# Later places for layer 1's gate products, and activations stored cell by cell in DRAM

## The chip, the cores and the metric

The kernel runs on one core of a Trainium2 chip. The metric is the device time of one execution in microseconds (us); lower is better. The core has a matrix engine (PE, with its weight loads shown as PEld), a vector engine (DVE), an activation engine (ACT), a general engine (POOL) and a sequencer that issues all transfers of this kernel (SP). Sixteen DMA engines carry the transfers between DRAM and the on-chip memory.

## The reference, cut to what matters

Two layers of a streaming encoder run over 2048 prompt frames and 32 sample frames of width 1024, all in f32.

```python
# layer 0
h  = rms_norm(x, ln_pre[0])
qa, ka, va, ga, qb, kb, vb, gb = split(h @ w_in_ab)        # 3328 columns
oa = window_attention(rope(qa), rope(ka), va, sinks)       # own 64-frame chunk + 2 before
ob = band_attention(qb, kb, vb, relpos)                    # own chunk + 8 before
x2 = x + rms_norm(concat(oa * silu(ga), ob * silu(gb)) @ w_out_ab, ln_post[0])
# layer 1
xb, z = split(rms_norm(x2, ln_pre[1]) @ w_in_c)            # 2048 columns
xc = causal_conv4(xb)
r  = sigmoid(blockdiag(xc, wa) + ba);  gi = sigmoid(blockdiag(xc, wx) + bx)   # the gates
a  = exp(8 * r * log_sigmoid(lam))
hs = scan(h[t] = a[t] * h[t-1] + sqrt(1 - a[t]**2) * gi[t] * xc[t])
y  = x2 + rms_norm((hs * silu(z)) @ w_out_c, ln_post[1])
```

Besides `y` the kernel returns the key, value, convolution and scan states.

## The kernel before, in words

**Data.** Activations lie transposed: the 1024 features are 8 groups (k) of 128 partitions, the frames run along the free axis. The 2084 columns (2048 prompt, 4 of padding, 32 sample) are cut into six blocks of 352 columns (the last has 324), and three parts `b` = 0, 1, 2 of two blocks each. Every f32 operand of a large product is split into a high and a low piece (`r0h`/`r0l`, `r1h`/`r1l` for activations, `wh`/`wl` for weights), so one output tile `acc` of 128 features by one block takes 8 x 3 = 24 matmuls.

**Stages.** Input projection of layer 0 for the three parts, with the attention of earlier parts mixed in; output projection of layer 0 (`out_part`, about 990 to 1180 us in the profile); then layer 1, part by part: `in_part` (16 weight tiles by two blocks, with gates, scan and so on), followed by its `out_part`. The last `out_part` ends the program.

**Cells.** Norms and residuals work on cells, half a block wide: 176 columns (162 in the last block). `norm_proc` loads cells of the input (`xT`) or of layer 0's result (`x2T`), squares them on ACT, reduces on DVE, sums over partitions by two matmuls into `misc`, and writes the high and low pieces. `fin_out` follows each `acc` of an output projection: ACT writes the scaled `acc` into the buffer `m` (two buffers, each 8 k by 352 columns) and its square, DVE adds the squares into `sacc`; after the eighth, `m` is multiplied by the norm factor `r`, the residual cell (loaded by `res_load` into `xr`, `eti` or `xt`) is added, and the cell goes to DRAM: to `x2T` in layer 0, to `yT` in layer 1. A buffer `m` is free for the next block only when these stores have landed. In DRAM `xT`, `x2T` and `yT` are matrices of 1024 rows by 2084 columns, so a cell of 176 columns is 1024 pieces of 704 bytes (`x_load`, and the stores in `add`).

**Gates.** In `in_part`, for each of eight feature groups `c`, `fin_x` copies `acc` to `xb`, DVE makes the convolution, ACT or DVE and DVE make the split operands `xs` (two tiles, one for each half of 128 features), and PE multiplies each by the gate weights `gh`, `gl` into `g` (4 matmuls for each tile). ACT takes tanh of `g`, then exp and sqrt; DVE continues to the scan. The waits are on rings of one or two buffers, so the channels follow one another.

**What sets the order.** The order of every engine's instructions is made at build time by a list scheduler (`Sched`). Each step is a generator that yields a request `R(engines, inputs, rings)`; the scheduler keeps estimated times for each engine, each tile (`sch.w`), the transfers (`dma_us`, from the length of the contiguous runs) and takes a step when its inputs are estimated ready. On the chip every engine runs its list strictly in order and waits on semaphores. So an estimate never makes a wait by itself; it decides what stands in front of what. SP issues in one list, too.

**Output weights of the last part.** The last `out_part` runs block by block, so that each weight tile is read twice from DRAM (`wh<-wo1s`, `wl<-wo1s`, 512 KB each, three buffers of each); its 16 tiles of 24 matmuls are the end of the program, but for the last norm.

Of the kernel before, what the change touches and what calls it, by code (L numbers as in the profile page):

```python
# [12 lines left out]
OP = mybir.AluOpType  # L13
# [3 lines left out]
KT = 8  # L17
# [35 lines left out]
WIN = 3.4133  # L53

# [346 lines left out]
def hybrid_kernel(ctx, tc, I, O):  # L401
# [30 lines left out]
    oT, zT, x2T = dt("oT", [D, TOK]), dt("zT", [D, TOK]), dt("x2T", [D, TOK])  # L432
# [191 lines left out]
    def split_R(xt, w, ri, col, ins=()):  # L624

        hh, hl = RT[ri]
        cs = slice(col, col + w)
        yield R("A", [xt] + list(ins))
        A.copy(hh[:, :, cs], xt[:, :, :w])
        th = sch.t["A"] + 0.13  # L630
        ends = []
        for ks in (slice(0, 4), slice(4, 8)):
            e, _ = yield R(("V", "G"), [lambda: th], cost=(0.8, 1.63))
            ENG[e].tensor_tensor(hl[:, ks, cs], xt[:, ks, :w], f32(hh[:, ks, cs]), OP.subtract)
            ends.append(sch.t[e] + 0.13)
        return max(ends)
# [29 lines left out]
    def norm_proc(src, b, gi, ri, key, rings, free=None, after=None, src_ready=(), then=None, blocks=(0, 1), hold=None):  # L666
# [5 lines left out]
        def block(bi, xs):  # L672
            cc = cells[2 * bi:2 * bi + 2]
            sa, sb = yield R("A", [xs[0]], [ssr, ssr])
            offs = [0, cc[0][3]]
            tot = cc[0][3] + cc[1][3]
            for x, (_, _, _, w), o in zip(xs, cc, offs):
                for ss, ks in ((sa, slice(0, 4)), (sb, slice(4, 8))):
                    sq, = yield R("A", [x], [sqr])
                    A.activation(sq[:, :, :w], x[:, ks, :w], AF.Square)  # L680
                    yield R("V", [sq])
                    V.tensor_reduce(ss[:, o:o + w], sq[:, :, :w].rearrange("p k t -> p t k"), AX.X, OP.add)
                    sqr.release(sq)
            e, _ = yield R(("G", "V"), [sa, sb], cost=(0.89, 0.43))
            ENG[e].tensor_tensor(sa[:, :tot], sa[:, :tot], sb[:, :tot], OP.add)
            ssr.release(sb)
            ps = yield from norm_sum(sa[:, :tot])
            r = sa
            yield R("A", [ps], func="sqrt")
            A.activation(r[:, :tot], ps[:, :tot], AF.Sqrt, bias=epsT, scale=1.0 / D)  # L690
            psr_.release(ps)
            for x, (_, _, _, w), o in zip(xs, cc, offs):
                yield R("V", [r])
                V.reciprocal(r[:, o:o + w], r[:, o:o + w])
                for k0 in (0, 4):
# [941 lines left out]

    def fin_out(S, c, acc, rel, cs):
        if c == 0:
# [4 lines left out]
        A.activation(S.m[:, c, cs], acc[:, cs], AF.Copy, scale=vec[:, S.gi, c:c + 1])  # L1644
# [16 lines left out]
        blk = 2 * S.b + S.bi  # L1661
# [20 lines left out]
        def add(o, sw, tm):  # L1682

            cc = slice(o, o + sw)
            for ks in parts:
# [28 lines left out]
        for o, sw in pieces:  # L1714
# [11 lines left out]
    def res_load(S):  # L1726
# [3 lines left out]
        if S.cells is LAST:  # L1730

            xa, = yield R("SP", rings=[xtr])
            xb, = yield R("SP", rings=[xrr])
            at = 0
            for o, sw in LAST:
                x = xb if o else xa
                S.xt[o] = x.rearrange("p k t -> p (k t)")[:, at:at + KT * sw].rearrange("p (k t) -> p k t", k=KT)
                at = at + KT * sw if o else 0
                x_load(S.xt[o], S.residual, T0[2 * S.b + S.bi] + o, sw)
# [97 lines left out]
    def in_part(b, base, ri, yi):  # L1837
# [4 lines left out]
        def fin_x(c, bi, acc):  # L1842
# [39 lines left out]
            for h, xt in enumerate(xs):  # L1882
                p_, = yield R("PE", [xt, ("gw", b, c)], [gr[h]])
# [181 lines left out]
def _layout(inputs):  # L2065
# [4 lines left out]
    xT[:, S0:] = a["x_sample"][0].T  # L2070
    nat = lambda n: [i * 128 + np.arange(128) for i in range(n)]
    gw = np.zeros((8, 128, 2, 128), f)
    for c in range(8):
# [22 lines left out]
        "xT": xT,  # L2096
# [15 lines left out]
_OUTS = {"yT": (1024, T0[5]), "yL": (128, KT * BW[5]), "akp": (128, 128), "avp": (128, 128), "bkp": (512, 512), "bvp": (512, 512),  # L2112
# [40 lines left out]
```

## Time and profile before

| | |
|---|---|
| median of 3 runs | 1818.16 us (1817.07 to 1822.6) |
| the profiled execution, its own time | 1822.39 us |
| its span, first to last instruction | 1820.6 us |
| PE busy in the span | 1732.4 us (95%) |
| DVE busy | 1544.3 us (85%) |
| ACT / POOL busy | 990.9 us (54%) / 324.8 us (18%) |
| DMA | 362.79 MB, 16 engines 66% busy on the queue of SP's transfers |
| granted TensorE clock, mean | 0.988 |

Busy times are unions of instruction times. A gap is put down to the engine or transfer that released the waiting instruction. All instructions carry the line of one helper (L103), so groups are told apart by tile names: `acc<-r0h,wh` writes tile `acc` and reads `r0h` and `wh`. The window view gives, for a stretch of time, each engine's busy time with the number of its instructions, the granted clock (1.00 is full), the mean busy share of the 16 DMA engines (it can pass 1 in a short stretch, since a packet counts where it starts) and the bytes moved in GB/s. DMA issues stand under SPq with the time that SP spent issuing.

### The profile page before, as it was taken

The page shows a single profiled execution, that of the slowest core. Times are in us where ns is not written, and L with a number is a line of the kernel's source. Part 1 is how long each engine was busy: PE and PEld are TensorE (multiplying, and loading weights), DVE is VectorE, ACT ScalarE, POOL GpSimd, SP SyncE. Part 2 cuts the span into 40 slices and gives each one's busy share as a digit, 9 for nine tenths or more (in the row PEclk, how much of TensorE's full clock was granted, in tenths as well). Part 3 has the DMA queues.
Part 4 walks back from the last instruction along what each step waited for, and adds up shares of the span by engine and source line. Part 5 has one row for each costly group of instructions (what it writes and reads, how often), then busy time and mean ns, then how long its engine had stood idle before and what let it go on. Part 6 is the DMA issues. An engine that isn't in the chain of part 4 may idle for free. (4 is left out here: it accounts for less than half of the span.)

```text
span 1820.6 us, 31699 instructions
## 1 busy us (share of the span) xinstructions
PE 1732.4 (95%) x11078; PEld 1673.4 (92%) x11078; DVE 1544.3 (85%) x3240; ACT 990.9 (54%) x2029; POOL 324.8 (18%) x283
## 2 busy tenths in 40 slices
PE   8999999999999999999998999998999999999996
PEld 7998999998899999899997999998899999999996
DVE  9899977899998779998887688899998989789844
ACT  4275543377666416666564333457854676437831
POOL 4332204323222233312114000000021000200001
PEclk8999999999999999999999999999999999999998
DMA  5798766888655369877867785785457733564376
GB/s 179 207 250 252 225 190 198 224 217 254 175 162 151 97 183 251 209 210 200 232 161 216 222 215 158 223 281 193 171 211 233 222 124 125 181 215 163 131 254 206
DMA packets 293367, 362.79 MB, mean 199 GB/s; under 512 B 38404, under 2 KB 244152, under 8 KB 293192
## 3 DMA queue, kind: packets, MB, share of 16 engines
q1 hardware_dynamic: 293208, 360.78, 66.2%
q8 instruction: 87, 1.43, 0.3%
q14 instruction: 72, 0.59, 0.1%
HBM read 255.77 MB, written 107.00 MB: 199 GB/s over the span
## 5 line engine op out<-in xcount | busy, mean ns | idle before, releaser
L103 PE MATMUL acc<-r0h,wh 128*128 128x352 f32 (+2 forms) x1832 | 592.9, 324 | 12.2 <-ACT r0h L103 5.6
L103 PE MATMUL acc<-r0l,wh 128*128 128x352 f32 (+2 forms) x1832 | 593.2, 324 | 2.8 <-DVE r0l L103 2.8
L103 PE MATMUL acc<-r0h,wl 128*128 128x352 f32 (+2 forms) x1832 | 592.7, 324 | 1.8 <-DMA wl<-wo1s 1.8
L103 PEld LDWEIGHTS acc<-r0h,wh 128*128 128x128 f32 x1832 | 347.1, 189 | 15.4 <-ACT r0h L103 6.5
L103 PEld LDWEIGHTS acc<-r0l,wh 128*128 128x128 f32 x1832 | 347.6, 190 | 4.9 <-DVE r0l L103 3.8
L103 PEld LDWEIGHTS acc<-r0h,wl 128*128 128x128 f32 x1832 | 347.4, 190 | 3.6 <-DMA wl<-wo1s 2.6
L103 PE MATMUL acc<-r1h,wh 128*128 128x352 f32 (+1 forms) x864 | 278.7, 323 | 3.5 <-ACT tz L103 1.8
L103 PE MATMUL acc<-r1h,wl 128*128 128x352 f32 (+1 forms) x864 | 278.4, 322 | 2.9 <-DVE wl L103 2.9
L103 PE MATMUL acc<-r1l,wh 128*128 128x352 f32 (+1 forms) x864 | 278.1, 322 | 0.0
L103 ACT ACTIVATE pt<-pt,nm 128x256 f32<-128x256 f32 (+6 forms) x272 | 169.7, 626 | 67.5 <-DVE nm L103 65.0
L103 POOL TENSOR_TENSOR wl<-wst,wh 128x1024 fp32r<-128x1024 f32 x41 | 101.7, 2481 | 465.5 <-DMA wst<-wo_in 346.1
L103 ACT CAST pp<-T 128x256 fp32r<-128x256 f32 (+4 forms) x314 | 132.8, 438 | 75.1 <-PE T L103 63.4
L103 PEld LDWEIGHTS acc<-r1h,wh 128*128 128x128 f32 x864 | 163.2, 189 | 4.6 <-ACT tz L103 2.1
L103 PEld LDWEIGHTS acc<-r1h,wl 128*128 128x128 f32 x864 | 163.1, 189 | 3.8 <-DVE wl L103 3.8
L103 POOL TENSOR_SCALAR pt<-pt,rr 128x256 f32<-128x256 f32 (+4 forms) x142 | 98.0, 700 | 384.1 <-DVE rr L103 219.1
L103 PEld LDWEIGHTS acc<-r1l,wh 128*128 128x128 f32 x864 | 163.2, 189 | 0.0
L103 DVE TENSOR_TENSOR pp<-T,pp 128x256 fp32r<-128x256 f32 (+4 forms) x314 | 151.3, 498 | 9.1 <-ACT pp L103 7.3
L103 PE MATMUL T<-ident,pt 128*128 128x128 f32 (+1 forms) x864 | 142.7, 273 | 14.2 <-DVE pp L103 10.8
L103 PE MATMUL O<-pp,vt 128*128 128x256 f32 (+2 forms) x728 | 133.9, 306 | 10.6 <-DVE pp L103 5.4
L103 PEld LDWEIGHTS T<-ident,pt 128*128 128x128 f32 (+1 forms) x864 | 99.9, 139 | 40.7 <-DVE pp L103 17.6
L103 ACT ACTIVATE m<-acc,vec 128x352 f32<-128x352 f32 (+2 forms) x89 | 48.9, 549 | 144.3 <-PE acc L103 138.4
L103 PE MATMUL S<-kk,qa 128*128 128x320 f32 (+5 forms) x376 | 121.3, 337 | 4.1 <-DVE nm L103 2.3
(242 smaller groups left out, 3055.4 us busy)
## 6 DMA issues: line engine op xcount, KB each, us to landing
wst<-w_in SPq DMA_DIRECT2D x93, 512.0 KB, 4.7
wst<-wo_in SPq DMA_DIRECT2D x32, 512.0 KB, 4.3
wh<-w1s SPq DMA_DIRECT2D x32, 512.0 KB, 3.6
wl<-w1s SPq DMA_DIRECT2D x32, 512.0 KB, 4.7
wh<-wo1s SPq DMA_DIRECT2D x24, 512.0 KB, 3.7
wl<-wo1s SPq DMA_DIRECT2D x24, 512.0 KB, 4.6
kk<-kB SPq DMA_DIRECT2D x32, 320.0 KB, 5.1
vt<-vB SPq DMA_DIRECT2D x16, 640.0 KB, 4.8
```

The source lines that it names most:

```text
L103: r = fn(*a, **k)
```

## The change

Two things are changed together. First, a gate's matmuls are offered to the scheduler 1.0 us later than the estimated end of their operand `xs` (`GLATE`). Second, `xT`, `x2T` and `yT` are stored in DRAM by cells, each partition's part of a cell in one piece: a cell of 176 columns is then 128 pieces of 8 x 176 x 4 = 5632 bytes. The two blocks that are loaded first get a copy of their own by blocks (`xF`), with pieces of 2816 bytes in place of 1408. On chip, `m` is laid out cell by cell as well; ACT's write of a whole block into it has two runs of 176 columns, and in the last block, whose cells are now 176 and 148 wide, it becomes two instructions. The last block's residual is loaded as two cells rather than three pieces, and the final sums of its second cell go to another tile (`xt`) than the residual's. The host arranges input and output accordingly.

```diff
+GLATE = 1.0
+SUBS = [[(0, 176), (176, 176)]] * 5 + [[(0, 176), (176, 148)]]
...
+    x2T = dt("x2T", [128, KT * TOK])
...
     def x_load(xt, src, t0, w):
-        SP.dma_start(out=xt[:, :, :w], in_=src[:, t0:t0 + w].rearrange("(k p) t -> p k t", p=128))
+        SP.dma_start(out=flat(xt)[:, :KT * w], in_=src[:, KT * t0:KT * (t0 + w)])
...
-        A.activation(S.m[:, c, cs], acc[:, cs], AF.Copy, scale=vec[:, S.gi, c:c + 1])
+        if cs == slice(0, BLK):
+            A.activation(flat(S.m).rearrange("p (x k t) -> p x k t", x=2, k=KT)[:, :, c], acc[:, cs].rearrange("p (x t) -> p x t", x=2),
+                         AF.Copy, scale=vec[:, S.gi, c:c + 1])
+        else:
+            for o, sw in subs(blk):
+                a, e = max(o, cs.start), min(o + sw, cs.stop)
+                if a < e:
+                    A.activation(m_cell(S.m, blk, a, e - a)[:, c], acc[:, a:e], AF.Copy, scale=vec[:, S.gi, c:c + 1])
...
-                    SP.dma_start(out=S.dst[:, T0[blk] + o:T0[blk] + o + sw].rearrange("(k p) t -> p k t", p=128), in_=m[:, :, cc])
+                    t = KT * (T0[blk] + o)
+                    SP.dma_start(out=S.dst[:, t:t + KT * sw].rearrange("p (k t) -> p k t", t=sw), in_=mc)
...
-                p_, = yield R("PE", [xt, ("gw", b, c)], [gr[h]])
+                tx = sch.w[xt.tensor.name] + GLATE
+                p_, = yield R("PE", [lambda: tx, ("gw", b, c)], [gr[h]])
```

Since both edits change the scheduler's estimates, the order differs from PE's row 657 of 9962 on; three places follow, before and after apart. (The helper's line is L103 before and L106 after.)

**SP's list near the end**, in the last `out_part`: `wo1s_115` and `wo1s_116` are the last two weight tiles, `yT_out<-m` are the two cells of the block before the last, `chp` to `ccs` small states. Before:

```order
L103 DMA yT_out<-m_10500 128x8x176 x2
L103 DMA wh_119<-wo1s_115 128x1024
L103 DMA wl_122<-wo1s_115 128x1024
L103 DMA chp_out<-hcar 128x8
L103 DMA chs_out<-hsmp 128x8
L103 DMA ccp_out<-hist 128x24
L103 DMA ccs_out<-csmp 128x24
L103 DMA wh_120<-wo1s_116 128x1024
L103 DMA wl_123<-wo1s_116 128x1024
L103 DMA xt_151<-x2T 128x8x176
```

After:

```order
L106 DMA wh_119<-wo1s_115 128x1024
L106 DMA wl_122<-wo1s_115 128x1024
L106 DMA chp_out<-hcar 128x8
L106 DMA chs_out<-hsmp 128x8
L106 DMA ccp_out<-hist 128x24
L106 DMA ccs_out<-csmp 128x24
L106 DMA yT_out<-m_10500 128x1408
L106 DMA wh_120<-wo1s_116 128x1024
L106 DMA wl_123<-wo1s_116 128x1024
L106 DMA yT_out<-m_10500 128x1408
L106 DMA xt_151<-x2T 128x1408
```

The two stores of `yT` stood ahead of the last two weight tiles; now one stands behind the first of these and one behind the second.

**PE's list in layer 0's output projection**, where `norm_proc` for layer 1's first block sums its squares (`misc<-xs,onesr`). Before:

```order
L103 MATMUL acc_159<-r1h,wl_124 128x352
L103 MATMUL misc_160<-xs_10567,onesr 128x352 x2
L103 MATMUL acc_159<-r1h,wh_121 128x352
L103 MATMUL acc_159<-r1l,wh_121 128x352
L103 MATMUL acc_159<-r1h,wl_124 128x352
L103 MATMUL acc_159<-r1h,wh_121 128x352
```

After:

```order
L106 MATMUL acc_0_10557<-r1h,wh_121 128x352
L106 MATMUL acc_0_10557<-r1l,wh_121 128x352
L106 MATMUL acc_0_10557<-r1h,wl_124 128x352
L106 MATMUL acc_0_10557<-r1h,wh_121 128x352
L106 MATMUL misc_160<-xs_10567,onesr 128x352 x2
L106 MATMUL acc_0_10557<-r1l,wh_121 128x352
```

The sum stood at row 5802, twelve matmuls before the end of an `acc` tile; it now stands at row 5818, four matmuls into the next tile: 16 rows later.

**PE's list in layer 1, second part**, one channel's gates (`g_0`, `g_1` by the first and second `xs` tile) among the products of the next weight tile. Before:

```order
L103 MATMUL acc_158<-r1h,wl_124 128x352
L103 MATMUL g_0_10559<-xs_10567,gh_10564 128x352
L103 MATMUL g_0_10559<-xs_10567,gl_10565 128x352
L103 MATMUL g_0_10559<-xs_10567,gh_10564 128x352
L103 MATMUL g_0_10559<-xs_10567,gl_10565 128x352
L103 MATMUL acc_0_10557<-r1h,wh_119 128x352
L103 MATMUL acc_0_10557<-r1l,wh_119 128x352
```

After:

```order
L106 MATMUL acc_0_10557<-r1h,wh_119 128x352
L106 MATMUL acc_0_10557<-r1l,wh_119 128x352
L106 MATMUL g_0_10559<-xs_10567,gh_10564 128x352
L106 MATMUL g_0_10559<-xs_10567,gl_10565 128x352
L106 MATMUL g_0_10559<-xs_10567,gh_10564 128x352
L106 MATMUL g_0_10559<-xs_10567,gl_10565 128x352
L106 MATMUL acc_0_10557<-r1h,wl_122 128x352
```

The first four stood at row 7800 and stand at 7808, behind eight matmuls of the next tile; the other four (by `xs_10568`) went from row 7812 to 7824.

More of the change, by code (lines that the diff above doesn't have):

```diff
@@ L431, in hybrid_kernel @@
     vAs, vBs = dt("vAs", [160, 2, 128]), dt("vBs", [544, 8, 128])
-    oT, zT, x2T = dt("oT", [D, TOK]), dt("zT", [D, TOK]), dt("x2T", [D, TOK])
+    oT, zT = dt("oT", [D, TOK]), dt("zT", [D, TOK])
+    x2T = dt("x2T", [128, KT * TOK])
     WSEQ = []
@@ L633, in split_R @@
             e, _ = yield R(("V", "G"), [lambda: th], cost=(0.8, 1.63))
-            ENG[e].tensor_tensor(hl[:, ks, cs], xt[:, ks, :w], f32(hh[:, ks, cs]), OP.subtract)
+            ENG[e].tensor_tensor(hl[:, ks, cs], xt[:, ks], f32(hh[:, ks, cs]), OP.subtract)
             ends.append(sch.t[e] + 0.13)
@@ L697, in block @@
                     for k in range(k0, k0 + 4):
-                        V.scalar_tensor_tensor(x[:, k, :w], x[:, k, :w], vec[:, gi, k:k + 1], r[:, o:o + w], OP.mult, OP.mult)
+                        y = dense(x, w)[:, k]
+                        V.scalar_tensor_tensor(y, y, vec[:, gi, k:k + 1], r[:, o:o + w], OP.mult, OP.mult)
             ssr.release(sa)
@@ L1682, in add @@
         def add(o, sw, tm):
[L1684 removed]
+            mc = m_cell(m, blk, o, sw)
             for ks in parts:
@@ L1730, in res_load @@
         if S.cells is LAST:
+            t0, (_, (ob, wb)) = T0[2 * S.b + S.bi], subs(2 * S.b + S.bi)
             xa, = yield R("SP", rings=[xtr])
-            xb, = yield R("SP", rings=[xrr])
-            at = 0
[L1735 to L1739, printed above, removed]
+            x_load(xa, S.residual, t0, ob)
+            S.xt[0] = dense(xa, ob)
+            S.xk[0] = sch.dma_end
+            xb, xo = yield R("SP", rings=[xrr, xtr])
+            x_load(xb, S.residual, t0 + ob, wb)
+            S.yt = {0: S.xt[0]}
+            at = 0
+            for o, sw in LAST[1:]:
+                S.xt[o] = dense(xb, wb)[:, :, o - ob:o - ob + sw]
+                S.yt[o] = flat(xo)[:, at:at + KT * sw].rearrange("p (k t) -> p k t", t=sw)
+                at += KT * sw
                 S.xk[o] = sch.dma_end
@@ L2095, in _layout @@
     return {
-        "xT": xT,
+        "xT": np.ascontiguousarray(np.concatenate([x3[:, :, T0[i] + o:T0[i] + o + w].reshape(128, KT * w) for i in range(6) for o, w in SUBS[i]], 1)),
+        "xF": np.ascontiguousarray(np.concatenate([x3[:, :, T0[i]:T0[i] + BLK].reshape(128, KT * BLK) for i in range(2)], 1)),
         "w0": _wtiles(a["w_in_ab"][0], _colperm0()),
@@ L2130 @@
     c = np.ascontiguousarray
-    yT = np.concatenate([g["yT"]] + [g["yL"][:, KT * o:KT * (o + w)].reshape(128, KT, w).transpose(1, 0, 2).reshape(1024, w) for o, w in LAST], 1)
+    cell = lambda y, o, w: y[:, KT * o:KT * (o + w)].reshape(128, KT, w).transpose(1, 0, 2).reshape(1024, w)
+    yT = np.concatenate([cell(g["yT"], T0[i] + o, w) for i in range(5) for o, w in SUBS[i]] + [cell(g["yL"], o, w) for o, w in LAST], 1)
     def kT(x, h, n):
```

35 lines of the change are left out of this document (23 added, 12 removed).

## The prediction

> **What bounds the kernel now.** I read the page first, for the engines.
>
> ```profile
> span 1820.6 us, 31699 instructions
> PE 1732.4 (95%) x11078; PEld 1673.4 (92%) x11078; DVE 1544.3 (85%) x3240; ACT 990.9 (54%) x2029; POOL 324.8 (18%) x283
> ```
>
> PE is busy 95% of the span, and its work isn't changed: the same matmuls by the same widths. So the change can only move what PE loses: 1820.6 - 1732.4 = 88 us idle, plus the stretches at a lower clock. What matters is where PE waits and for whom. Next, therefore, the table of waits and the users of `x2T`:
>
> ```profile
> PE g L103 <- DVE xs L103: 8.2, 11, 1.7
> PE acc L103 <- ACT r0h L103: 5.6, 3, 3.5
> ...
> who waited for it (us, times):
>   ACT m L103: 8.7, 3
>   ACT sq L103: 5.8, 2
> ```
>
> The first row is what the later gates aim at: PE waited 11 times, 8.2 us, for the gates' operand. The last rows say that the layout matters too: ACT stood still 8.7 us for stores to `x2T` to free `m`, and 5.8 us for loads from it.
>
> **How fast cells move.** Of a transfer I need the time on all 16 DMA engines, since its followers wait for that where the engines are full. The first two windows hold only 704-byte pieces (loads of `x2T`), the third rows of 5 KB into 64 partitions (`kk<-kB`), the fourth only weight tiles (4 KB in each of 128 partitions), the fifth the first loads, with pieces of 1408 bytes:
>
> ```profile
> 1367.00:1370.00 3.00, 3.00 (x20) 3.00 (x20) 3.00 (x3) 1.09 (x3) 1.17 (x1) 1.00 0.89 177
> 1417.50:1420.50 3.00, 3.00 (x21) 3.00 (x20) 2.80 (x5) 0.81 (x2) 0.00 (x0) 1.00 0.76 222
> 542.00:545.00 3.00, 3.00 (x23) 2.98 (x22) 2.85 (x10) 1.90 (x5) 0.72 (x1) 1.00 0.73 178
> 1750.00:1753.00 3.00, 3.00 (x20) 3.00 (x19) 0.45 (x1) 0.91 (x2) 0.00 (x0) 1.00 0.99 344
> 10.50:13.50 3.00, 3.00 (x11) 2.90 (x11) 3.00 (x4) 1.45 (x2) 3.00 (x4) 0.50 1.06 366
> ...
> wst<-wo_in SPq DMA_DIRECT2D x32, 512.0 KB, 4.3
> x2T<-m SPq DMA_DIRECT2D x10, 704.0 KB, 7.3
> ```
>
> GB/s over share gives the pace of full engines: 199 and 292 for 704-byte pieces, 244 for `kk`, 347 for weights, 345 for the first loads. A cell is 704 KB = 721 kB: 2.5 to 3.6 us now. In pieces of 5632 bytes it should take 2.1 us if it goes like the weights, 3.0 us if like `kk`. I take the weights, whose 128 partitions are those of a cell; `kk` fills 64. So a cell saves 0.4 to 1.5 us, at worst it loses 0.5. From issue to landing the two last rows set 7.3 us for a store against 4.3 us for 512 KB in long pieces; scaled by size that is 4.3 + 192/347 = 4.9 us, about 2.4 us sooner. SP is held up as well:
>
> ```profile
> 1088.84 5.11 SPq L103 DMA_DIRECT2D xt<-x2T  x2
> 1742.57 0.32 SPq L103 DMA_DIRECT2D wh<-wo1s  x1
> 1785.95 3.33 SPq L103 DMA_DIRECT2D wh<-wo1s  x1
> ```
>
> An issue that takes 0.32 us with nothing before it took 3.33 us behind two cells, and two cells took 5.11 us. With 128 pieces for a cell in place of 1024 I expect this to go.
>
> The Trainium skill speaks against the whole edit: by "DMA: Bandwidth & Descriptors", section "Specifications", pieces of 512 bytes or more already run at line rate, so 704 would do. By it the layout's terms below would be zero. The windows above disagree: 199 to 292 against 347.
>
> **Term 1, layer 0's output projection: 9.5 us won.** Windows, then PE's and ACT's instructions with their waits in brackets:
>
> ```profile
> 1100.00:1110.00 10.00, 7.20 (x29) 6.64 (x28) 7.98 (x10) 3.49 (x8) 0.00 (x0) 0.69 0.72 222
> 1150.00:1160.00 10.00, 7.32 (x44) 7.03 (x44) 10.00 (x23) 6.57 (x12) 0.00 (x0) 0.92 0.65 191
> 1160.00:1170.00 10.00, 10.00 (x61) 10.00 (x61) 9.19 (x14) 7.18 (x10) 0.00 (x0) 0.91 0.71 218
> ...
> 1088.20 0.43 PE L103 MATMUL acc<-r1h,wh 128*128 128x352 f32 x1 [1.83 <-ACT tz L103]
> 1104.65 1.22 PE L103 MATMUL misc<-xs,onesr 128*128 128x352 f32 x2 [2.80 <-DVE xs L103]
> 1158.96 0.64 PE L103 MATMUL acc<-r0h,wh 128*128 128x324 f32 x1 [2.68 <-ACT tz L103]
> ...
> 1075.03 0.55 ACT L103 ACTIVATE m<-g,vec 128x352 f32<-128x352 f32 x1 [4.57 <-DMA x2T<-m]
> 1093.95 0.79 ACT L103 ACTIVATE sq<-ex 128x704 f32<-128x704 f32 x1 [3.58 <-DMA ex<-x2T]
> 1145.19 0.56 ACT L103 ACTIVATE m<-g,vec 128x352 f32<-128x352 f32 x1 [3.79 <-DMA x2T<-m]
> ```
>
> Three waits of PE, 7.3 us, each follow a wait of ACT for a store or load of `x2T`, 12 us in all. After two of them the clock is halved for a while: 0.31 x 10 = 3.1 us lost at 1100, (0.08 + 0.09) x 10 = 1.7 us at 1150 to 1170. Together 12.1 us. The first: the store lands about 2.4 us sooner, half of ACT's 4.57, and I count 1.5 of 1.83. The second: PE's list now has the sum 16 rows later, and a full-speed matmul takes 0.165 us (112.85 us for 684, row below), so 2.6 us of the 2.80 go by the order alone, and its load is faster too; with the clock 2.8 + 3.1, I count 5.5. The third depends on a store and then on a weight tile behind the stores; 2.5 of 2.68 + 1.7. Bounds: 2.6 (the place in the list alone, no clock) to 12.1.
>
> **Term 2, the last output projection: 7 us won, 0.7 given back.** Here DMA is the bound:
>
> ```profile
> 1768.00:1771.00 3.00, 1.83 (x7) 1.59 (x8) 1.31 (x3) 1.18 (x1) 0.00 (x0) 0.74 1.03 415
> 1771.00:1774.00 3.00, 3.00 (x16) 3.00 (x16) 1.10 (x1) 0.56 (x1) 0.00 (x0) 0.69 0.31 124
> 1795.00:1798.00 3.00, 2.02 (x8) 1.79 (x9) 0.00 (x0) 0.00 (x0) 0.00 (x0) 0.80 0.93 306
> 1798.00:1801.00 3.00, 3.00 (x16) 3.00 (x15) 0.00 (x0) 0.00 (x0) 0.00 (x0) 0.64 1.12 296
> ...
> 1768.52 0.39 PE L103 MATMUL acc<-r0h,wh 128*128 128x324 f32 x1 [1.59 <-DMA wh<-wo1s]
> 1769.70 0.64 PE L103 MATMUL acc<-r0h,wl 128*128 128x324 f32 x1 [0.66 <-DMA wl<-wo1s]
> 1795.25 0.39 PE L103 MATMUL acc<-r0h,wh 128*128 128x324 f32 x1 [1.82 <-DMA wh<-wo1s]
> 1796.51 0.44 PE L103 MATMUL acc<-r0h,wl 128*128 128x324 f32 x1 [0.73 <-DMA wl<-wo1s]
> ...
> 1807.46 1.25 DVE L103 RECIPROCAL r<-r 128x176 f32<-128x176 f32 x1 [4.45 <-ACT r L103]
> 1808.73 0.33 ACT L103 ACTIVATE r<-misc,epsT 128x84 f32<-128x84 f32 x1 [0.54 <-PE misc L103]
> ```
>
> At 1768 PE waits 2.25 us for a weight tile that two residual cells delayed, and then runs slow: 3 x (0.26 + 0.31) = 1.7 us. Two cells save 0.8 to 3.0 us; I count 1.2, which leaves a wait of 1 us and, I think, the full clock: 2.9. At 1795 it is 2.55 us for the tile that stood behind two stores of `yT` in SP's list, and 3 x (0.20 + 0.36) = 1.7 us of clock. That tile is now ahead of the stores, so all 4.2 should go. What is late next there is the last tile, behind one store: 721 kB at 347 GB/s, 2.1 us, while a tile of 24 matmuls lasts 24 x 0.165 = 4 us, so it is covered. All four gaps whose clock I count, of 2.25 to 2.8 us, were followed by a slow stretch, in all 3.1 + 1.7 + 1.7 + 1.7 = 8.2 us. The Trainium skill's "TensorE: Matmul & The Clock Gate", section "Why this matters for your kernels", has the clock drop only after gaps of some 3 us; by it these stretches would not come from the gaps, and the sum would be up to 8 us less. The trace disagrees, and I go by it.
>
> The tail after PE's end is a chain on DVE. There ACT writes the first 240 columns of `m` in two instructions, the norm's sums stand four short matmuls later, and DVE's second instruction is the reciprocal of the last 84 columns, which needs the ACT result that ended at 1809.06, where DVE was free at 1808.71: 0.35 + some 0.35 us, 0.7 lost. Bounds of the term: 3 to 7.9.
>
> **Term 3, the gates: 3 us won.** Two windows, the gates of the first and of the second part:
>
> ```profile
> 1210.00:1345.00 135.00, 124.55 (x761) 121.17 (x760) 130.08 (x182) 104.05 (x131) 4.82 (x2) 1.00 0.62 213
> 1428.00:1546.00 118.00, 112.85 (x684) 108.97 (x684) 104.85 (x151) 85.81 (x110) 0.00 (x0) 1.00 0.44 143
> ```
>
> A gate moves 4 to 12 rows, 0.7 to 2 us, and the 8.2 us of waits would go. But who waits for a gate: ACT's tanh, then DVE's scan, in line. In the first part DVE is busy 130.08 of 135 us (96%) where PE is at 124.55; a wait taken from PE there comes back at the part's end, where PE already waits for the last `r0h` and `r0l`. In the second part DVE has 11% left (104.85 of 118). I count the waits of the second and third part, some 5 us, less 2 us more at the three ends. Bounds: all 8.2 won; or every one of 24 channels late by 0.7 us and in line, 16.8 lost less 8.2, so 8.6 lost.
>
> **Costed at nothing.** The two-run write of `m` by ACT and the doubled one of the last block, 13 + 2 more instructions of some 0.4 us: ACT is at 54%, and PE has two other `acc` tiles to go to. The first loads, at 345 GB/s already: 0 to 1. The rest of layer 0 is reordered from PE's row 657 on, without a direction that a row would show: 0, with 5 us either way:
>
> ```profile
> 115.00:956.00 841.00, 816.66 (x5462) 778.06 (x5461) 729.71 (x1957) 481.73 (x1197) 219.79 (x210) 1.00 0.72 202
> ```
>
> PE idles 24.3 us there. From the whole I take 2.8 us, since DVE (85%) comes next and will keep something of each wait.
>
> **Sum.** 9.5 + 7.1 - 0.7 + 3 - 2.8 = 16 us. The profiled execution took 1822.4 us (1.8 us outside its span), 4.2 us over the median of the runs; the terms are differences within one execution, and I take them from the median: 1818.2 - 16 = 1802.
>
> **Rivals.** (a) The length of the pieces buys nothing: full engines carry a cell as slowly as before. Then what remains is order: the sum's later place (2.6), the tile ahead of the stores (4.2 - 0.7), the gates (3), and 1 us of SP's time: 1808. The two 704-byte windows and the landing times speak against it. (b) The gates' delay runs through: DVE's line of channels is full, as the 96% says, and the 8.6 us are lost in place of 3 won: 1802 + 11.6 = 1814. The 11% in the second part speak against it. (c) The slower side: the reordered attention. Its operands pass PE, ACT, DVE and PE again, and PE's idle 24.3 us in 115 to 956 could double, if transposes meet products that are not ready; 1802 + 24 = 1826. It decides from 16 us of added idle time; nothing in the rows asks for it, but nothing excludes it. (d) Long pieces go at `kk`'s pace or worse: a cell takes 3.0 us, 0.5 more than the faster of today's windows and 0.6 less than the slower; term 1 falls to 4, the first wait of term 2 stays: 1811.
>
> **How the numbers follow.** My forecast has 56% (1794 to 1809: term 1 and 2 between their bounds, mostly), (a) 15%, (b) 13%, (c) 7%, (d) 7%; 2% lie below 1794. About 0.3%, 5.4 us, is what a measurement of this kernel can tell from no change. Faster takes my case, what lies below it, (a), most of (d) and a third of (b): 0.82; same the rest of (b) and of (d): 0.11; slower is (c): 0.07. The range goes to 1790 below and 1816 above, past (a), (d) and (b).
>
> **What would show it.** Right: no wait of ACT for `x2T<-m` over 2 us, `x2T<-m` and `xr<-x2T` landing within 5 us, no issue of SP over 1 us behind cells, no wait for `wo1s` at the last two tiles, the clock at 1.00 from 1000 us to the end of PE, and PE's waits for `xs` under 3 us. Wrong: cell transfers under 250 GB/s at full share, longer waits for `r0h` at the ends of the parts, or PE idle well over 24 us between 115 and 956 us.

## The result, and the profile after

The changed kernel takes 1810.39 us (median of 5 runs, 1805.5 to 1813.68) against 1818.16 us for the kernel before: ratio 0.9947, 95% interval 0.9928 to 0.9966. So it is faster, by 7.8 us by the medians and 9.6 by the ratio, where 16 were forecast, and the time lies inside the forecast range (1790 to 1816) and 8 us over the forecast itself (1802). The profiled execution is the median one. From its page and its table of waits (in the latter: total us, times, longest):

```profile
span 1808.6 us, 31683 instructions
PE 1726.3 (95%) x11078; PEld 1674.2 (93%) x11078; DVE 1537.9 (85%) x3228; ACT 1001.9 (55%) x2055; POOL 322.1 (18%) x285
...
PE acc L106 <- ACT r0h L106: 10.3, 3, 4.6
PE g L106 <- DVE xs L106: 8.5, 6, 5.0
ACT m L106 <- DMA x2T<-m: 10.2, 3, 9.4
```

PE waits for `xs` about as long as before (8.5 us, where it was 8.2), in 6 waits instead of 11, and for `r0h` 10.3 instead of 5.6 us. Neither the wait for `xs` nor ACT's wait for `m` (10.2 us, where it was 8.7), with which the prediction began, fell. What did fall is seen in layer 0's output projection and at the end. Windows (busy time of PE, PEld, DVE, ACT, POOL, granted clock, DMA share, GB/s), then SP's, ACT's and PE's instructions with their waits in brackets:

```profile
1100.00:1110.00 10.00, 8.62 (x54) 8.32 (x53) 8.36 (x15) 4.58 (x8) 0.00 (x0) 1.00 0.35 125
1150.00:1160.00 10.00, 10.00 (x65) 9.86 (x64) 9.86 (x25) 7.88 (x19) 0.00 (x0) 1.00 0.49 195
1090.00:1092.00 2.00, 2.00 (x15) 2.00 (x14) 1.57 (x4) 0.13 (x1) 0.00 (x0) 1.00 0.99 406
1066.50:1068.50 2.00, 2.00 (x14) 2.00 (x14) 2.00 (x3) 0.00 (x0) 0.00 (x0) 1.00 0.99 299
...
x2T<-m SPq DMA_DIRECT2D x11, 704.0 KB, 4.1
...
1782.95 0.38 SPq L106 DMA_DIRECT2D yT_out<-m  x1
...
1074.48 0.56 ACT L106 ACTIVATE m<-g,vec 128x352 f32<-128x352 f32 x1 [9.36 <-DMA x2T<-m]
...
1105.92 0.43 PE L106 MATMUL misc<-xs,onesr 128*128 128x352 f32 x1 [1.38 <-DVE xs L106]
1789.25 0.38 PE L106 MATMUL acc<-r0h,wl 128*128 128x240 f32 x1 [0.84 <-DMA wl<-wo1s]
```

At 1100 and 1150 us the clock is full, where it was 0.69 and 0.92. Full DMA engines now carry cells at 410 GB/s when they are loaded (406 over 0.99; 199 to 292 before) and at 300 where a store and a load run together (1066.5 us): 1.8 to 2.4 us for a cell. A store lands after 4.1 us instead of 7.3, and its issue takes 0.3 to 0.4 us. Of the waits for the last two weight tiles 0.84 us is left. What got worse most lies in the first part of layer 1:

```profile
1232.90 0.66 PE L106 MATMUL g<-xs,gh 128*128 128x352 f32 x1 [4.99 <-DVE xs L106]
1333.83 0.66 PE L106 MATMUL acc<-r0h,wh 128*128 128x352 f32 x1 [3.90 <-ACT r0h L106]
1335.30 0.66 PE L106 MATMUL acc<-r0l,wh 128*128 128x352 f32 x1 [0.81 <-DVE r0l L106]
...
1230.00:1240.00 10.00, 7.10 (x30) 6.91 (x31) 9.55 (x14) 6.80 (x10) 0.00 (x0) 0.66 0.34 82
1332.00:1342.00 10.00, 7.36 (x29) 6.99 (x30) 7.10 (x7) 4.47 (x8) 2.76 (x2) 0.66 0.36 131
```

One gate waits 4.99 us, the part's end 4.7 us, and after each the clock is halved (these matmuls take 0.66 us each, and the clock's mean over the 10 us is 0.66).

**A ledger for PE.** To compare all profiles I use one number per stage: for each PE instruction the distance from its start to the next one's start, less the median distance for that shape in the profile of before (0.160 us for 352 columns), summed over a stage. I call it the excess; it holds waits and slow clock together. Stages are cut at equal sums of the nominal distances and named by before's times: 91–300 is the early attention, 1006–1183 layer 0's output projection, the next three columns are the parts of layer 1, and the last is the last output projection. In the stages left out, up to 91 and from 300 to 1006 us, all 14 profiles lie within 2.8 and 4.1 us of one another.

| kernel | 91–300 | 1006–1183 | 1183–1384 | 1384–1582 | 1582–1731 | 1731–end | span |
|---|---|---|---|---|---|---|---|
| before, first profile | 11.0 | 14.2 | 13.2 | 9.5 | 4.5 | 11.8 | 1820.6 |
| before, second profile (e8_before) | 9.2 | 9.3 | 13.2 | 9.2 | 4.4 | 9.4 | 1808.1 |
| changed | 14.8 | 2.4 | 19.8 | 8.8 | 2.0 | 3.8 | 1808.6 |
| gates alone (e1_gates) | 8.7 | 10.2 | 12.0 | 8.3 | 3.4 | 5.7 | 1805.7 |
| gates alone, old end (e11_gates_end) | 8.3 | 10.7 | 12.1 | 7.9 | 4.0 | 7.9 | 1806.6 |
| layout alone (e2_layout) | 12.6 | 2.5 | 14.8 | 9.4 | 4.4 | 4.4 | 1806.0 |
| layout, old estimates (e3_oldprice) | 8.7 | 4.9 | 19.2 | 10.0 | 3.7 | 5.7 | 1806.2 |
| new estimates, old layout (e4_order) | 15.3 | 9.0 | 23.0 | 16.2 | 4.1 | 6.4 | 1829.5 |
| before, two stores moved (e10_behind) | 8.1 | 13.5 | 13.2 | 9.5 | 4.1 | 5.4 | 1809.0 |
| changed, two stores moved back (e12_ahead) | 16.6 | 2.3 | 19.7 | 8.5 | 1.8 | 7.5 | 1812.4 |
| changed, old estimates in attention (e5_mix) | 9.2 | 2.5 | 20.1 | 10.5 | 1.8 | 3.9 | 1805.1 |
| changed, gates late in parts 2, 3 only (e6_late_b12) | 13.0 | 3.0 | 14.5 | 9.0 | 2.1 | 4.0 | 1801.5 |
| both of the last (e9_best) | 8.9 | 2.3 | 15.5 | 8.3 | 2.0 | 4.0 | 1798.1 |
| changed, DVE relieved (e7_relief) | 13.2 | 2.4 | 21.2 | 9.1 | 2.1 | 3.9 | 1808.6 |

### The profile page after: what moved, and what is told of

Its sections match the earlier page's. It is cut to its first block, busy times and chain, and to the rows that moved or that the text cites. A ratio compares the mean times of both kernels' runs of the same rounds, so it can differ in the third digit from the quotient of the medians.

```text
span 1808.6 us, 31683 instructions
## 1 busy us (share of the span) xinstructions
PE 1726.3 (95%) x11078; PEld 1674.2 (93%) x11078; DVE 1537.9 (85%) x3228; ACT 1001.9 (55%) x2055; POOL 322.1 (18%) x285
## 5 line engine op out<-in xcount | busy, mean ns | idle before, releaser
L106 PE MATMUL acc<-r0h,wh 128*128 128x352 f32 (+2 forms) x1832 | 592.8, 324 | 11.5 <-ACT r0h L106 10.3
L106 PE MATMUL acc<-r0l,wh 128*128 128x352 f32 (+2 forms) x1832 | 593.1, 324 | 2.1 <-DVE r0l L106 2.0
L106 PE MATMUL acc<-r0h,wl 128*128 128x352 f32 (+2 forms) x1832 | 592.6, 323 | 2.3 <-DMA wl<-wo1s 1.6
L106 PEld LDWEIGHTS acc<-r0h,wh 128*128 128x128 f32 x1832 | 347.1, 189 | 14.0 <-ACT r0h L106 11.2
L106 PEld LDWEIGHTS acc<-r0l,wh 128*128 128x128 f32 x1832 | 347.1, 189 | 4.4 <-DVE r0l L106 3.4
L106 PEld LDWEIGHTS acc<-r0h,wl 128*128 128x128 f32 x1832 | 347.0, 189 | 4.3 <-DMA wl<-wo1s 2.4
L106 PE MATMUL acc<-r1h,wh 128*128 128x352 f32 (+1 forms) x864 | 277.9, 322 | 0.6 <-ACT xb L106 0.6
L106 PE MATMUL acc<-r1h,wl 128*128 128x352 f32 (+1 forms) x864 | 277.7, 321 | 0.0
L106 PE MATMUL acc<-r1l,wh 128*128 128x352 f32 (+1 forms) x864 | 277.6, 321 | 0.0
L106 ACT ACTIVATE pt<-pt,nm 128x256 f32<-128x256 f32 (+6 forms) x272 | 170.3, 629 | 70.0 <-DVE nm L106 68.9
L106 ACT CAST pp<-T 128x256 fp32r<-128x256 f32 (+4 forms) x314 | 133.1, 439 | 74.2 <-PE T L106 62.2
L106 POOL TENSOR_SCALAR pt<-pt,rr 128x256 f32<-128x256 f32 (+5 forms) x144 | 99.3, 699 | 397.5 <-DVE rr L106 183.4
L106 PEld LDWEIGHTS acc<-r1h,wh 128*128 128x128 f32 x864 | 162.7, 188 | 0.9 <-ACT xb L106 0.9
L106 PEld LDWEIGHTS acc<-r1l,wh 128*128 128x128 f32 x864 | 162.8, 188 | 0.0
L106 PEld LDWEIGHTS acc<-r1h,wl 128*128 128x128 f32 x864 | 162.6, 188 | 0.2 <-DVE wl L106 0.2
L106 DVE TENSOR_TENSOR pp<-T,pp 128x256 fp32r<-128x256 f32 (+4 forms) x314 | 151.3, 498 | 8.6 <-ACT pp L106 6.7
L106 PE MATMUL T<-ident,pt 128*128 128x128 f32 (+1 forms) x864 | 141.7, 274 | 15.5 <-DVE pp L106 12.5
L106 PE MATMUL O<-pp,vt 128*128 128x256 f32 (+2 forms) x728 | 133.8, 307 | 8.7 <-DVE pp L106 5.8
L106 PEld LDWEIGHTS T<-ident,pt 128*128 128x128 f32 (+1 forms) x864 | 100.2, 139 | 40.6 <-DVE pp L106 20.0
L106 ACT ACTIVATE m<-acc,vec 128x352 f32<-128x352 f32 (+3 forms) x103 | 51.1, 511 | 141.3 <-PE acc L106 135.6
L106 PE MATMUL S<-kk,qa 128*128 128x320 f32 (+5 forms) x376 | 121.5, 337 | 4.5 <-issue 1.5
L106 PEld LDWEIGHTS O<-pp,vt 128*128 128x128 f32 x728 | 104.5, 189 | 13.0 <-DVE pp L106 7.1
```

The costliest lines, as they stand in the source:

```text
L106: r = fn(*a, **k)
```

## The experiments

Ratios are of timed runs to those of the kernel before on the same chip, with 95% intervals. Differences in us are the ratio's distance from 1 times 1818 us.

### Which of the two edits, and list or transfers

**e1_gates**, the gates alone, on the kernel before:

```diff
+GLATE = 1.0
-                p_, = yield R("PE", [xt, ("gw", b, c)], [gr[h]])
+                tx = sch.w[xt.tensor.name] + GLATE
+                p_, = yield R("PE", [lambda: tx, ("gw", b, c)], [gr[h]])
```

> The kernel before with the gates' later place alone (GLATE = 1.0); cells stay in 704-byte pieces and the estimates of transfers are as before. Theory A (the gates' delay hands PE's waits on to the part ends, and faster cells carry the gain): layer 1 loses the 4.4 us that it lost in the changed kernel, and nothing else moves: about 4 us slower, 1822; waits for xs fall, waits for r0h at the three part ends grow from 5.6 us. Theory B (the gates gain what they aim at, and layer 1 lost by the list that the new transfer estimates made): some 3 us faster, 1815, with r0h waits at the part ends as before. Under either the output projections (1001 to 1183 us, and 1730 to the end) keep their excess of 14.2 and 11.8 us.

Measured: ratio 0.9967 (0.9952 to 0.9983), 6 us faster. From its waits, where before it read 8.2 us in 11 waits:

```profile
PE g L104 <- DVE xs L104: 0.3, 1, 0.3
```

The later place does what it says, and theory A falls: layer 1 does not lose. But the excess from 1183 us to 1731 shrinks only from 27 to 24 us. The last projection, which no gate touches, goes from 11.8 and 9.4 to 5.7: the scheduler put one of two stores of `yT` a tile earlier in SP's list. e11_gates_end tests that.

**e2_layout**, the layout alone (the changed kernel with the gates' line of before):

> The changed kernel with GLATE = 0: the layout alone, with the estimates that follow from it. Theory A: the gain of the two output projections (11.8 + 8 us) less the 3 us lost in the attention, without the 4.4 us lost in layer 1: about 4 us faster than the changed kernel, 1806; the single wait for xs in the first part stays under 3 us and the r0h waits at the part ends are near 5.6 us. Theory B: layer 1 loses as much or more, since the gates' delay won something there: 1810 to 1814.

Measured: 0.9943 (0.9930 to 0.9957), 10 us faster, no different from both edits together (0.9947). On top of the layout the gates' delay brings nothing measurable: it takes 2.4 us from the third part and adds 5.0 to the first (14.8 to 19.8).

**e3_oldprice**, the layout with the scheduler's estimates of 704-byte pieces, and gates as before:

```diff
+    names = (out.tensor.name, src.tensor.name)
+    if any(n.startswith(("x2T", "xT", "yT", "yL")) for n in names):
+        run = min(run, 176)
+    if any(n.startswith("xF") for n in names):
+        run = min(run, 352)
     return total / run * (0.016 + run * 4 / 23e3) / 16
```

> The layout with the gates as before, and with the scheduler told that a cell still moves in 704-byte pieces: fast transfers, and lists near the old ones (459 of some 9960 rows of PE differ from the kernel before, since the last block's cells are 176 and 148 wide now). Theory A (length of the pieces carries the gain): waits of ACT for x2T and of PE for wo1s shrink without a new list; of the two projections' excess of 26 us some 6 + 6 us go, so about 1806. Theory O (the list carries it): the cells' speed is hidden, 1816 to 1818, and PE still waits over 2 us at the last two weight tiles and for the sum misc.

Measured: 0.9955 (0.9942 to 0.9969), 8 us faster. In layer 0's output projection the waits of ACT that the prediction quoted with 4.57, 3.58 and 3.79 us read:

```profile
1084.56 0.80 ACT L111 ACTIVATE sq<-ex 128x704 f32<-128x704 f32 x1 [2.38 <-DMA ex<-x2T]
1131.55 0.56 ACT L111 ACTIVATE m<-g,vec 128x352 f32<-128x352 f32 x1 [1.66 <-DMA x2T<-m]
```

The first is gone, and PE's excess is 4.9 us there, for 9.3 to 14.2 in five profiles with slow cells and the old list. So the length of the pieces carries most of this term. Theory A had about 12 us in all, theory O 2 at most.

**e4_order**, the old layout with estimates of long pieces:

```diff
+    names = (out.tensor.name, src.tensor.name)
+    if any(n.startswith(("x2T", "xT", "yT")) for n in names):
+        run = total // 128
     return total / run * (0.016 + run * 4 / 23e3) / 16
```

> The kernel before in its old layout, with the scheduler told that a cell moves in 5632-byte pieces: the new kind of list, and slow transfers (434 rows of PE differ from the changed kernel's list). Theory A: the sum's later place and the weight tile ahead of the stores win some 3 + 4 us, the waits for stores and loads of x2T stay, the attention's new list costs 3 us: about 1814. Theory O: the list does it all, 1806 to 1808, with the excess of both projections under 5 us.

Measured: 1.0064 (1.0047 to 1.0082), 12 us slower, which neither theory had: theory A's 1814 missed by 15 us. A list made for faster transfers than there are is worse than the old one. Its largest piece, in the first part of layer 1:

```profile
1237.29 0.66 PE L106 MATMUL g<-xs,gh 128*128 128x352 f32 x1 [2.55 <-DVE xs L106]
1247.14 0.66 PE L106 MATMUL acc<-r1h,wl 128*128 128x352 f32 x1 [5.88 <-DVE wl L106]
...
1237.00:1251.00 14.00, 7.53 (x24) 6.52 (x25) 13.71 (x21) 10.36 (x12) 0.00 (x0) 0.51 0.25 68
```

DVE is full there (13.71 of 14 us), PE waits twice and runs at half clock for the whole stretch. The opposite error, e3_oldprice's, still gives 8 us. Why DVE is late at just that tile I did not follow further back.

### Where the layer-0 and layer-1 losses come from

**e5_mix**: the changed kernel, with e3's estimates until the attention is done (the same two conditions, guarded).

```diff
+DENSE = []
...
+    if not DENSE and any(n.startswith(("x2T", "xT", "yT", "yL")) for n in names):
+        run = min(run, 176)
...
+    DENSE.append(1)
     sch.set(("attention",))
```

> The changed kernel, but the scheduler is told until the end of the attention that a cell moves in 704-byte pieces, and the true 5632 after it: the old kind of list while the attention runs, the new one behind it. Theory L (the attention's new list, made from the shorter estimates, costs some 4 us between 91 and 300 us: PE's excess over its nominal spacing there was 14.8 and 12.6 us in the two kernels with both the new list and the layout, 15.3 with the new list alone, against 11.0, 8.7 and 8.7 with the old kind of list): about 4 us under the changed kernel, 1803 to 1806. Rival D (those differences are only what one execution differs from another): the same as the changed kernel, 1808 to 1811, with an excess of some 13 us in that stretch.

Measured: 0.9928 (0.9911 to 0.9944), 13 us under before. The stretch reads, in before, in its second profile, in the changed kernel and in e9_best, which has the same list there as e5_mix:

```profile
91.00:306.00 215.00, 208.84 (x1347) 201.34 (x1346) 184.11 (x456) 117.94 (x298) 56.20 (x58) 1.00 0.75 220
```

```profile
91.00:306.00 215.00, 210.17 (x1359) 203.28 (x1358) 185.89 (x457) 118.10 (x298) 56.88 (x57) 1.00 0.74 220
```

```profile
91.00:306.00 215.00, 204.43 (x1323) 197.85 (x1323) 182.50 (x449) 116.14 (x294) 55.73 (x59) 1.00 0.74 218
```

```profile
91.00:306.00 215.00, 210.10 (x1362) 203.49 (x1361) 185.58 (x460) 118.48 (x298) 57.42 (x58) 1.00 0.74 221
```

PE does some 24 to 39 instructions less there with the new list (x1323 against x1347 to x1362), at equal DMA share. In the ledger the old kind of list gives 8.1 to 11.0 us in eight profiles, the new one 12.6 to 16.6 in six: theory L holds, 5 us in the ledger. In the timed runs the step from the changed kernel is 3.5 us, with intervals that overlap.

**e6_late_b12**: the changed kernel, the gates as before in the first part.

```diff
-                tx = sch.w[xt.tensor.name] + GLATE
+                tx = sch.w[xt.tensor.name] + (GLATE if b else 0.0)
```

> The changed kernel with the gates' later place in the second and third part alone. Theory G (in the first part DVE is full, so that the gates' delay there comes back as the 3.90 + 0.81 us wait at the part's end and the slow clock behind it; in the other parts it wins): some 4 us under the changed kernel, 1805 to 1807, PE's excess from 1236 to 1384 us falls from 19.9 to 14 or 15. Rival D (the list of the first part is bad with the layout whatever the gates do): 1808 to 1811, and the excess there stays at 18 or more.

Measured: 0.9929 (0.9914 to 0.9943); excess from 1183 to 1384 us 14.5 instead of 19.8 us. Its waits at the places of the changed kernel's 4.99, 3.90 and 0.81:

```profile
1236.11 0.43 PE L106 MATMUL g<-xs,gl 128*128 128x352 f32 x1 [2.29 <-DVE gl L106]
1239.40 0.43 PE L106 MATMUL acc<-r1h,wl 128*128 128x352 f32 x1 [1.58 <-DVE wl L106]
1242.64 0.40 PE L106 MATMUL g<-xs,gh 128*128 128x352 f32 x1 [0.75 <-DVE gh L106]
...
1329.57 0.43 PE L106 MATMUL acc<-r0h,wh 128*128 128x352 f32 x1 [1.26 <-ACT r0h L106]
1330.83 0.43 PE L106 MATMUL acc<-r0l,wh 128*128 128x352 f32 x1 [0.83 <-DVE r0l L106]
...
1230.00:1240.00 10.00, 6.13 (x37) 5.55 (x37) 9.90 (x17) 3.82 (x6) 0.00 (x0) 1.00 0.05 14
```

Here PE waits 4.62 us around 1236 us, in the changed kernel 4.99: nearly the same. In three pieces it leaves the clock full, in one piece it is followed by half clock. (In e9_best the first of the same three pieces, 2.28 us, was followed by 3.41 us of half clock, so the pieces do not always escape it.) And the wait at the part's end is 2.6 us shorter. Theory G's figures hold; its reason, a full DVE, this run does not show. In time it is 3.3 us under the changed kernel, again with intervals that overlap.

**e7_relief**: in the first part, the copies for `xs` and `wh` fixed on ACT.

```diff
-            e, xs = yield R(("A", "V"), [xc], [xsr, xsr], cost=(1.3, 0.87))
+            e, xs = yield R(("A", "V") if b else ("A", "A"), [xc], [xsr, xsr], cost=(1.3, 0.87))
-            e, (h, l) = yield R(("A", "V"), [("wst", i), ...
+            e, (h, l) = yield R(("A", "A") if WSEQ[i][0] == "w1" else ("A", "V"), [("wst", i), ...
```

> The changed kernel with some 10 us of DVE's work in the first part of layer 1 given to ACT: the copies that make the high piece of the gates' operand and of that part's weights. Theory F (DVE is what limits the first part, at 96%): PE's excess from 1236 to 1384 us falls by some 6 to 10 us from 19.9, the time to 1801 to 1805. Rival C (it is the chain of one channel after another, and ACT's copies are slower, 1.3 us for 0.87 in the scheduler's own costs): the same or slower, 1810 to 1816, with PE waiting for xs and r0h as long or longer.

Measured: 0.9978 (0.9965 to 0.9991), slower than the changed kernel if anything. Two waits in it:

```profile
1334.80 0.66 PE L106 MATMUL acc<-r0h,wh 128*128 128x352 f32 x1 [7.05 <-ACT r0h L106]
...
1210.00:1345.00 135.00, 120.59 (x717) 118.49 (x716) 123.78 (x175) 107.38 (x138) 1.51 (x1) 0.95 0.53 189
```

The waits inside the part shrink, and 7.05 us stand at its end. Theory F is not borne out: with the copies moved from DVE to ACT, the first part is not shorter. DVE is not cleared by this, since ACT's copies are longer (0.78 us for a copy of `xs`, DVE's 0.52, in the changed kernel's trace) and stand in the same chain. What stands at the part's end is the last `r0h`, which ACT writes; which step of the last channel's way through ACT and DVE is the late one was not tested.

### Two executions of one list

**e8_before**: the kernel before, once more.

> The kernel before once more, unchanged, for a second profile: what differs between two executions of one list. Theory S (the profile that the prediction was read from was a slow draw, 1822.4 us against a median of 1817 to 1818, and the extra sat in the slow clock behind waits): near 1817, with the same waits at the same instructions, and 3 to 6 us less of excess in the two output projections, where it was 14.2 and 11.8 us; one or two of the slow stretches at 1104, 1158, 1769 and 1797 us are missing or shorter. Rival T (the extra sat in layer 0): the two projections stay at 14 and 12 us.

Measured: one execution of 1809.88 us; the one profiled first took 1822.39. The lists are the same, and the waits stand at the same instructions. The sum and the `tz` wait, which read 2.80 and 2.68:

```profile
1097.93 1.22 PE L103 MATMUL misc<-xs,onesr 128*128 128x352 f32 x2 [2.26 <-DVE xs L103]
1150.41 0.41 PE L103 MATMUL acc<-r0h,wh 128*128 128x324 f32 x1 [1.96 <-ACT tz L103]
...
1150.00:1160.00 10.00, 9.59 (x62) 9.59 (x63) 9.90 (x16) 8.54 (x14) 0.00 (x0) 1.00 0.78 245
```

Theory S holds, though the time came out below what it expected: 4.9 + 2.4 of the 12.5 us lie in the two output projections, 1.8 in the early attention, 2.6 from 300 to 1006 us. After the wait of 1.96 us the clock stayed full.

### The end, by SP's list alone

**e10_behind**: the kernel before, with the stores of `yT` held behind the last two weight tiles. PE's, DVE's and ACT's lists are word for word those of before.

```diff
-                    yield R("SP", [lambda: th])
+                    yield R("SP", [lambda: th] + ([("wt", len(WSEQ) - (1 if o else 2))] if S.final else []))
```

> The kernel before, with only the two stores of yT moved in SP's list: the first stands behind the last weight tile but one, the second behind the last, as in the changed kernel; cells of 704-byte pieces, all other lists word for word as before. Theory O (at the end the place in the list carries the gain): the last projection's excess, 11.8 and 9.4 us in two profiles of the kernel before, falls by the 2.6 to 4.2 us of the last wait and its slow clock: 3 to 4 us faster, 1812 to 1813. Theory A (the stores are slow wherever they stand): PE waits as long for the last tile, behind one slow store; no change, 1815 to 1817.

**e12_ahead**: the changed kernel with the stores ahead of these tiles, the other three lists word for word as in the changed kernel (the key is set at the second store; the last residual loads are held behind the tiles in the same way).

```diff
-                wt[i] = h, l = yield R("SP", [("wt", i - 1), ("ws", x)], [whr, wlr])
+                wt[i] = h, l = yield R("SP", [("wt", i - 1), ("ws", x)] + [("stored",)] * (i == len(WSEQ) - 2), [whr, wlr])
```

> The changed kernel with only SP's list changed at the end: the two stores of yT ahead of the last two weight tiles, as in the kernel before; cells in 5632-byte pieces. Theory O: the two stores still delay the last tiles, by 1.7 to 1.9 us of full engines each; PE waits some 3 us there, with a slow stretch behind it 4 to 5 us slower, 1814 to 1815. Theory A (fast stores are harmless wherever they stand): at most 1 us slower, 1810 to 1811.

Measured: e10_behind 0.9980 (0.9966 to 0.9993), 3.6 us faster than before. e12_ahead 0.9979 (0.9969 to 0.9989), some 6 us slower than the changed kernel by the two ratios. The last tiles' waits, 1.82 + 0.73 in the first profile of before, in e10_behind and in e12_ahead:

```profile
1789.89 0.38 PE L103 MATMUL acc<-r0h,wl 128*128 128x240 f32 x1 [0.84 <-DMA wl<-wo1s]
```

```profile
1786.29 0.39 PE L106 MATMUL acc<-r0h,wh 128*128 128x324 f32 x1 [1.83 <-DMA wh<-wo1s]
1788.03 0.64 PE L106 MATMUL acc<-r0h,wl 128*128 128x324 f32 x1 [1.21 <-DMA wl<-wo1s]
```

Theory O holds in both: the place decides, with short pieces and with long. Long pieces ahead of the tiles still cost 3 us of waiting.

**e11_gates_end**: e1_gates, with the stores held where the kernel before has them; PE's, DVE's and ACT's lists are those of e1_gates.

```diff
-                    yield R("SP", [lambda: th])
+                    yield R("SP", [lambda: th] + ([("wt", len(WSEQ) - 3)] if S.final else []))
```

> The gates' later place on the kernel before, as in the first run, with the two stores of yT held where the kernel before has them: this leaves the gates alone, without what their new list did to the end. Theory E (most of what the gates' place alone won was the end's new order): of the 7 us under the kernel before some 2 to 3 stay, about 1814, with the last projection's excess at 9 to 12 us again and waits for xs under 1 us in all. Theory B (the gates themselves won it): 1809 to 1810, as in the first run.

Measured: 0.9982 (0.9972 to 0.9992), 3.3 us faster than before. The wait for `wh` of the last weight tile but one, which e1_gates does not have, is back:

```profile
1781.39 0.39 PE L104 MATMUL acc<-r0h,wh 128*128 128x324 f32 x1 [1.84 <-DMA wh<-wo1s]
```

The last projection's excess goes from 5.7 to 7.9 us. This speaks for theory E: of e1_gates' 6 us about half was the end of SP's list, by chance, though the two intervals overlap. The 3.3 us are the gates' own, on the old list.

### A faster version

**e9_best**: the edits of e5_mix and e6_late_b12 together.

> The two edits of the last pair together: old estimates until the attention is done, and the gates' later place in the second and third part alone. If the stretches add up (theory P: some 4 us in the attention's list, 5 us in the first part of layer 1, each seen alone): 1798 to 1801. If they don't (theory Q: what the attention's list wins is eaten by the wait for r0h at its end, or the first part's list comes out differently again): 1803 to 1806, like either alone.

Measured: 1800.52 us, 0.9901 (0.9884 to 0.9918), 18 us under before; its interval lies below that of the changed kernel (0.9928 to 0.9966). Either edit alone could not be told from the changed kernel by its interval; both together can, and they add up (9.6 + 3.5 + 3.3 make 16 us).

## Why the prediction was right and wrong

The time fell inside the range, but not all by the forecast's path: two terms held, one had the wrong sign in this kernel, and one that was put at nothing cost 5 us.

**Term 1, 9.5 us: right.** Five profiles with the old list and slow cells have 9.3 to 14.2 us there, mean 11.6; seven with the new list and fast cells 2.3 to 3.0, mean 2.5: 9.1 us. By e3_oldprice (4.9) the faster cells alone win 6.7 of them, by e4_order (9.0) the list alone 2.6. That the profile read from had the highest of the five did no harm, since not all of its 12.1 us were counted; how much to leave out was judgement, and that it came so close is in part luck. One step was argued wrongly: ACT's wait for the store did not go. In the changed kernel's list ACT is asked for that `m` sooner and stands 9.36 us, and PE has no wait over 0.7 us there; I take it that other `acc` tiles are free, which no run tests.

**Term 2, 7.1 less 0.7: nearly right in size.** 9.7 us in three profiles with the old end, 4.0 in six with the new one: 5.7 won. The split is near, too: 4.2 us were counted for the stores' place and 2.9 for the residual cells. In the ledger the place is worth 4.3 us with slow cells (e10_behind, 5.4) and 3.5 with fast ones (e12_ahead, 7.5), and the cells' speed 2.2 and 1.4. But the 2.9 us were read from one execution. In e10_behind, with slow cells and up to there the lists of before, PE waits 0.9 us behind the two residual cells where the prediction quoted 2.25, and the clock stays full:

```profile
1761.82 0.39 PE L103 MATMUL acc<-r0h,wh 128*128 128x324 f32 x1 [0.25 <-DMA wh<-wo1s]
1763.00 0.42 PE L103 MATMUL acc<-r0h,wl 128*128 128x324 f32 x1 [0.65 <-DMA wl<-wo1s]
```

The tail grew by 0.3 us, from 11.9 to 12.2.

**Term 3, 3 us won: right for the gates alone, of the wrong sign in this kernel.** Alone they win 3.3 us (1.5 to 5.1). In the changed kernel layer 1 loses 3.7 (first part 6.6 lost, second 0.5 and third 2.4 won); 2.0 of them came with the delay, since e2_layout has 28.6 us over the three parts and the changed kernel 30.6. The prediction had the mechanism, "a wait taken from PE there comes back at the part's end", and charged 2 us for three ends. At the end of the first part the kernel before has 2.51 us (1.47 in its second profile):

```profile
1339.00 0.43 PE L103 MATMUL acc<-r0h,wh 128*128 128x352 f32 x1 [1.67 <-ACT r0h L103]
1340.27 0.42 PE L103 MATMUL acc<-r0l,wh 128*128 128x352 f32 x1 [0.84 <-DVE r0l L103]
```

On the old list the delay brings nothing back there (0.29 us in e11_gates_end). With the layout it does: 2.09 to 2.11 us in the four profiles without the delay in that part (e2_layout, e3_oldprice, e6_late_b12, e9_best), 4.71 to 5.11 in three with it (the changed kernel, e12_ahead, e5_mix). And it costs more than its length, by the slow clock behind it, which the term did not count. That DVE's 96% was the reason is not borne out (e7_relief); why the delay comes back on one list and not on the other stays open. Nor is the delay all that can go wrong in that part: e3_oldprice, without it, has 19.2 us of excess there, with a wait of 3.31 us and half clock at 1263 us.

**The reordered attention, "0, with 5 us either way": this step failed.** It costs 5 us. It was said that no row shows a direction, and the chip shows one: this list is worse with either length of pieces (15.3 in e4_order). Rival (c) named the place and put its price at 24 us.

**The 2.8 us "kept by DVE"** were a guess that happened to cover part of this. The sum with measured terms: 9.1 + 5.7 - 0.3 - 3.7 - 5.0 = 5.8 us. The timed runs give 9.6 (6.2 to 13.1). The rest is not placed; with two executions of one list 12.5 us apart it can't be from one or two profiles.

**The rivals.** (a) falls: cells go at 300 to 410 GB/s, and e3_oldprice shows what that is worth. (d) falls with it. (b)'s place was right for the first part only. The figures of the three, 1808, 1811 and 1814, lie nearer to 1810 than the forecast, but not by their mechanisms.

**What was to be seen.** Right: cells well over 250 GB/s when loaded, stores of `x2T` landing after 4.1 us, SP's issues behind cells under 1 us, nearly no wait at the last tiles. Missed: ACT was not to wait over 2 us for `x2T<-m` (9.36), loads `xr<-x2T` were to land within 5 us (6.1 in the median), the clock was to be full from 1000 us on (it is halved at 1231, 1333 and 1542), and waits for `xs` were to stay under 3 us. The first sign named for "wrong", longer waits for `r0h`, came true. PE's idle time from 115 to 956 us, also named, rose from 24.3 to 28.0 us.

## What to carry to other kernels

Where a scheduler's estimates set the lists, a change of the estimates is a change of its own: try it with the old estimates (here 5 us were to be had back in a stage that the edit did not aim at), and fear estimates that are too short more than ones too long (here the first lost 12 us, and the second kept 8 of the layout's 10). Before a forecast is read from one execution, take a second profile of the same kernel; the waits repeat, their lengths and the half clock behind them vary. And a store that nobody waits for belongs behind the loads that someone does.

## What the runs showed of the hardware

**The clock is judged in fixed stretches of 3.413 us.** In all 14 profiles (by the granted clock that each records), until PE's end, each half-clock stretch begins on one grid of 3.413 us within its execution and lasts a whole number of its steps. Of the 87 full-clock steps in which PE was busy under 0.44 of the time, 86 were followed by a half one (the other, at 0.38, lies in the first 10 us of e9_best), and none in which it was busy over 0.59; between these both occur. So a wait of 1.9 us can halve the clock if it lies inside one step: e2_layout's of 1.90 us at 1266 us did, e8_before's of 1.96 us at 1150, which two steps share, did not, nor did e6_late_b12's three waits of 2.29, 1.58 and 0.75 us. The same wait in one list was followed by 6.83 us of half clock when it lasted 2.80 or 3.00 us, and by 3.41 us at 2.26, 2.43 and 2.81. The Trainium skill's "TensorE: Matmul & The Clock Gate", section "What's actually happening", has the free-running stretch of 3413 ns, and the runs agree. Its section "Why this matters for your kernels" has the clock drop after gaps of some 3 us, and by the runs 2 us are enough where they fall into one step.

**A packet costs 8 ns and its bytes.** In the traces of before and of the changed kernel, packets of 704, 1408, 2816, 4096 and 5632 bytes took 34, 60, 112, 159 and 215 ns in the median. All five lie on one line: 8 ns for each packet and 27.2 bytes per ns on its engine. At these times 16 full engines carry 331 GB/s in pieces of 704 bytes, 412 in 4096 and 419 in 5632; cells of 5632-byte pieces were loaded at 406 to 417. So 4-KB pieces are hardly slower than cells: the 347 GB/s that the prediction took for the weights come from a window in which the mean packet took 187 ns instead of 159.
